# Expert weights in pieces for both experts of a pair, the overflow loop behind the second pair, and the transposed intermediate copied by ScalarE

## The chip, the core and the metric

One Trainium2 chip; the kernel runs on one of its cores. The metric is device time in microseconds (us) of one execution. Engines: PE is TensorE, PEld its weight loads, DVE is VectorE, ACT is ScalarE, POOL is GpSimd, SP is SyncE, which here issues nearly all DMAs.

## What is computed

One encoder layer on 512 tokens of width 2048: four mixers side by side (a differential attention, a bidirectional RWKV7, a dilated attention, an S5 scan), an output projection, cross attention, and a two-level mixture of experts; then a final RMS norm. The change touches only the mixture of experts. The reference of that part, cut to what matters:

```python
def hier_moe(h, wr_group, wr_expert, w1, w3, w2):
    gp = softmax(xt @ wr_group)            # 4 groups, the best one is taken
    ep = softmax(el)                       # 8 experts of that group, the best TOP_K = 2 are taken
    gate = (g_w * top_w).reshape(-1)
    ...
    def run(args):
        xb, e = args
        return (jax.nn.silu(xb @ w1[e]) * (xb @ w3[e])) @ w2[e]
    ...
    out = jnp.zeros((t, d), F32).at[slot_tok].add(ys.astype(F32) * slot_gate[:, None])
```

There are 32 experts; w1 and w3 are 2048x512 each, w2 is 512x2048, all in f32. So 12.6 MB of weights belong to an expert, and 402.7 MB to the stage.

## The kernel before, in words

The mixers and the cross attention come first and take the first 1736 us. The stage of the experts follows, in class `Moe`. `Moe.columns` runs beside the cross attention: it collects the router's logits `lg` while the last columns of the residual `H` are made. `Moe.run` then routes (`moe_route`), counts the tokens that go beyond 64 of an expert (`moe_overflow`), computes the gates (`gates`), and works through the experts in 16 pairs, `pair(mp, i, rest)` for i = 0 to 15. Each expert gets 64 slots, so a pair fills 128 partitions of PSUM with two matmuls of 64 columns of stationary weights that share the array.

A pair has these parts, in the order in which PE does them:

- 32 steps over w1 and w3 (into PSUM tiles `p1` and `p3`, both named `ph`), each of two matmuls (one per expert) of a channel tile `X[q, kt]` of 128 channels with a weight tile 128x512. An f32 matmul of this kind shows as two records in the trace.
- At step 10 `spread`: the one-hot of the slots is transposed and the gates are picked.
- `s` = silu(p1) * p3 (ACT at step 24, DVE after the last step), four transposes of `s` on PE into `ps`, and a copy of the transposed intermediate to SBUF, `hT` (named `mo_h`), on DVE (line 2067).
- w2 in four column blocks c of 512 (tile `py`), each followed by `split` (ACT writes `mo_yh`, DVE `mo_yl`) and, one block later, by `scatter`: eight matmuls that add the slots' results to token rows, and four DVE adds into the accumulator `mo_A` (line 2074). The scatter of the last block is handed to the next pair as `rest` and runs there after step 1.

The channel tiles X of a quad of experts (two pairs) come from `gather(q, u)`, u = 0 to 7: 16 matmuls of f32r halves of H (`mo_hi` from ACT, `mo_lo` from DVE, made by `halves`, two buffers each) with the one-hot of the quad's slots (`slots4`, DVE, line 1969), into one PSUM buffer (`pse`), which DVE then copies to `mo_xT` (line 1995). Four gathers for the next quad lie in each pair: three at the steps in `GQ`, one between the last step and the transposes.

Weights come through `Chunks`: pieces of 2 MB, one DMA each on SP's queue, into five buffers `wch` that are used in turn. `Chunks.order` is the order of the pieces; a piece holds eight channel tiles of one expert (w1, w3) or two column blocks of one expert (w2). SP waits, piece by piece, until PE is done with the buffer that it will overwrite:

```python
self.order += [(wn, 2 * i + j, h) for h in range(2) for wn in (1, 3) for j in range(2)]
self.order += [(2, 2 * i + j, h) for h in range(2) for j in range(2)]
```

As each step needs both experts, two pieces are in use at a time and are released together.

`moe_rest` is a loop for tokens beyond 64 slots (`tc.For_i(0, total, 1)`, line 1750), run by all engines: each loads `total`, compares and branches. For the inputs timed here the trace shows no instruction of its body. It stands between the routing and pair 0. The instructions' order on each engine is set by a scheduler from the code's order, its own time estimates and priorities (`tc.high_priority`), within the blocks that the loop separates.

Of the kernel before, what the change touches and what calls it, by code (L numbers as in the profile page):

```python
# [22 lines left out]
P = 128  # L23
# [60 lines left out]
def layouts(I):  # L84

    def tiles(w):
        n = w.shape[1] // P
        return np.ascontiguousarray(w.reshape(KT, P, n, P).transpose(2, 1, 0, 3).reshape(n, P, KT * P))  # L90
# [4 lines left out]
    def experts(w):  # L95
        return np.ascontiguousarray(w.reshape(32, KT, P, 512).transpose(0, 2, 1, 3)).reshape(32, P, KT * 512)

    def par(a):
# [6 lines left out]
        "moe_w2": np.ascontiguousarray(I["moe_w2"][0].reshape(32, 4, P, 2, 2, 512).transpose(0, 3, 2, 4, 1, 5)).reshape(32, 2, P, 4096),  # L105
# [1542 lines left out]
GQ = ((4, 12, 20), (18, 22, 28))  # L1648
# [94 lines left out]
def moe_rest(k, tc, pool, PS, H, A, G, rstd, VAL, blocks, gm, iota):  # L1743

    nc, I = k.nc, k.I
    ps, psh, psy = PS
    cum, cux, total = blocks
    total = nc.values_load(total[0:1, 0:1], min_val=0, max_val=NOV,
                           skip_runtime_bounds_check_because="1024 places make at most 15 blocks beyond the first 64 of an expert")
    with tc.For_i(0, total, 1) as i:  # L1750

        ib = pool.tile([P, 1], F32, name="ov_ib")
        nc.vector.tensor_copy(ib, iota[:, bass.ds(i, 1)])
        mk = pool.tile([P, NE + 1], F32, name="ov_mk")
        m2 = pool.tile([P, NE], F32, name="ov_m2")
# [7 lines left out]
        nc.vector.tensor_tensor(m2, mk[:, 0:NE], iota[:, 0:NE], op=OP.mult)  # L1763
        ef = pool.tile([P, 1], F32, name="ov_ef")
        nc.vector.tensor_reduce(ef, m2, axis=AX.X, op=OP.add)
        ei = pool.tile([P, 1], I32, name="ov_ei")
        nc.vector.tensor_copy(ei, ef)
        e = nc.values_load(ei[0:1, 0:1], engines=(mybir.EngineType.SP,), min_val=0, max_val=NE - 1,
                           skip_runtime_bounds_check_because="an index into 32 experts")
        pr = pool.tile([P, NT, NE], F32, name="ov_pr")  # L1770
        vs = pool.tile([P, NT], F32, name="ov_vs")
        gf = pool.tile([P, 2, NT], F32, name="ov_gf")
        for src, dst in ((VAL, vs), (G, gf[:, 0])):
            nc.vector.tensor_tensor(pr, src, bc(mk[:, None, 0:NE], [P, NT, NE]), op=OP.mult)
            nc.vector.tensor_reduce(dst, pr, axis=AX.X, op=OP.add)
        nc.vector.tensor_copy(gf[:, 1], rstd)
        nc.vector.tensor_scalar(vs, vs, mk[:, NE:NE + 1], None, op0=OP.subtract)
        OH = pool.tile([P, NT, SLOT], F32, name="ov_OH")
        nc.vector.tensor_tensor(OH, bc(iota[:, None, 1:], [P, NT, SLOT]), bc(vs[:, :, None], [P, NT, SLOT]), op=OP.is_equal)
        X = pool.tile([P, KT, SLOT], F32, name="ov_X")  # L1780
# [5 lines left out]
        OT = pool.tile([SLOT, NT, P], F32R, name="ov_OT")  # L1786
# [7 lines left out]
        g = pool.tile([SLOT, 2], F32, name="ov_g")  # L1794
        nc.vector.tensor_copy(g, pg[0:SLOT])
        hh = []
        for wn in (1, 3):
            p = psh.tile([P, DFF], F32, name="ph")
            for kt in range(KT):
                w = pool.tile([P, DFF], F32, name="ov_w", bufs=2)  # L1800
                nc.sync.dma_start(w, I[f"moe_w{wn}"][bass.ds(e, 1)].rearrange("e p c -> p (e c)")[:, kt * DFF:kt * DFF + DFF])
                mm(nc, p[0:SLOT], X[:, kt], w, start=(kt == 0), stop=(kt == KT - 1))
            hh.append(p)
        s = pool.tile([SLOT, DFF], F32, name="ov_s")
# [5 lines left out]
        hT = pool.tile([P, 4, SLOT], F32, name="ov_h")  # L1810
        nc.vector.tensor_copy(hT, pt)
        for c in range(4):
            py = psy.tile([P, 512], F32, name="py")
            for kt in range(4):
                w = pool.tile([P, DFF], F32, name="ov_w", bufs=2)
                a = ((c % 2) * 4 + kt) * DFF
                nc.sync.dma_start(w, I["moe_w2"][bass.ds(e, 1), c // 2].rearrange("e p c -> p (e c)")[:, a:a + DFF])
                mm(nc, py[0:SLOT], hT[:, kt], w, start=(kt == 0), stop=(kt == 3))
            yh = pool.tile([SLOT, 512], F32R, name="ov_yh")
            yl = pool.tile([SLOT, 512], F32R, name="ov_yl")  # L1820
# [9 lines left out]
class Moe:  # L1830
    def __init__(self, k, ctx, pool, H, tmp):
# [9 lines left out]
        nc.gpsimd.iota(self.iota, pattern=[[1, SLOT + 1]], base=0, channel_multiplier=0, allow_small_or_imprecise_dtypes=True)  # L1841
        self.lg = mp.tile([P, NT, 8 + NE], F32, name="mo_lg")
# [14 lines left out]
    def columns(self, c, tmp, ps, wr, t):  # L1857
# [4 lines left out]
        if c + t == 0:  # L1862
# [3 lines left out]
            nc.vector.tensor_tensor(wr, wr, bc(k.V[:, a:a + KT][:, :, None], [P, KT, NR]), op=OP.mult)  # L1866
        if (c, t) == (1, 0):
# [37 lines left out]
    def run(self, out, mx2):  # L1905
# [28 lines left out]
        for i in range(NE // 2 - 1):  # L1934
            rest = self.pair(mp, i, rest)

# [43 lines left out]
    def gather(self, q, u, ps=None, more=True):  # L1980
# [13 lines left out]
        k0 = 2 * u  # L1994
        nc.vector.tensor_tensor(self.piece[:, k0 % 4:k0 % 4 + 2], px, bc(self.gm[:, k0:k0 + 2][:, :, None], [P, 2, 4 * SLOT]), op=OP.mult)  # L1995
        if more:
            for j in range(2):
                self.halves((k0 + 2 + j) % KT)
# [27 lines left out]
    def pair(self, mp, i, rest=None, done=None):  # L2026
# [9 lines left out]
        todo = [] if q == NE // 4 - 1 else [lambda u=u: self.gather(q + 1, u, None, (q, u) != (NE // 4 - 2, 7))  # L2036
# [134 lines left out]
```

## Time and profile before

| | |
|---|---|
| median of 3 runs | 2807.52 us (2806.95 to 2813.43) |
| the profiled execution | 2806.31 us |
| its span, first to last instruction | 2804.6 us |
| PE busy over the span | 2647.6 us (94%) |
| mean granted TensorE clock | 0.983 of full speed |
| DMA, mean over the span | 227 GB/s; in the last thousand us near 400 GB/s |

The span is what the views of the trace count from; 1.7 us of the profiled execution's time lie outside it. A view is read as follows: "idle" is the time in which an engine did nothing before an instruction, with what ended it; a window's row gives each engine's busy time in it, then the clock, the share of time in which the 16 DMA engines were busy, and what they moved. Times in a timeline are us from the span's start.

### The profile page before, as it was taken

To read this page: it belongs to the slowest core of one execution; us is meant where nothing else is said; L and a number is where in the kernel's file an instruction comes from. 1 tells how busy PE (TensorE), PEld (TensorE's weight loads), DVE (VectorE), ACT (ScalarE), POOL (GpSimd) and SP (SyncE) were. 2 spreads that over 40 slices of the span, in tenths; PEclk is the share of its full clock that TensorE was granted. 3 is DMA by queue.
4 is the path that set the end of the run, shared out by engine and by line. 5 is a ranking of instruction groups with operands and counts; after the bars stand their busy time and mean duration, and the time that the engine had idled before them with its cause. 6 is when DMAs were issued, how large, how long until landed. Compare 5 with 4: busy or idle time off the path is not lost. (4 is left out here: it accounts for less than half of the span.)

```text
span 2804.6 us, 43696 instructions
## 1 busy us (share of the span) xinstructions
PE 2647.6 (94%) x17978; PEld 1803.4 (64%) x17978; DVE 1381.3 (49%) x2426; ACT 911.5 (32%) x1668; POOL 246.4 (9%) x370
## 2 busy tenths in 40 slices
PE   7999999999899799999999998999999999999996
PEld 4787777777678688788788777444444444444433
DVE  8747474655486564565434344333333333333323
ACT  4134333433266454656423343211111111111103
POOL 5300010000137800000000000000000000000000
PEclk9999999999999999999999999999999999999998
DMA  4521122221646577667534242689999999999997
GB/s 154 197 97 62 63 70 72 66 81 56 153 143 203 168 203 208 211 203 225 185 113 117 90 165 83 271 367 389 397 395 370 416 378 419 372 415 387 414 411 278
DMA packets 157420, 635.77 MB, mean 227 GB/s; under 512 B 25376, under 2 KB 58784, under 8 KB 132512
## 3 DMA queue, kind: packets, MB, share of 16 engines
q1 hardware_dynamic: 157216, 632.93, 61.1%
q8 instruction: 143, 2.34, 0.3%
q14 instruction: 61, 0.50, 0.1%
HBM read 593.55 MB, written 39.32 MB: 226 GB/s over the span
## 5 line engine op out<-in xcount | busy, mean ns | idle before, releaser
L1034 DVE TENSOR_TENSOR wlo<-wraw,whi 128x512 fp32r<-128x512 f32 x556 | 399.4, 725 | 387.0 <-ACT whi L1033 380.6
L1033 ACT CAST whi<-wraw 128x512 fp32r<-128x512 f32 x556 | 339.2, 620 | 579.3 <-PE pj L158 472.6
L158 PE MATMUL ph<-wch,mo_xT 128*64 128x512 f32 x2048 | 471.6, 599 | 11.2 <-DMA wch<-in_moe_w_dram 11.2
L158 PEld LDWEIGHTS ph<-wch,mo_xT 128*64 128x64 f32 x2048 | 149.0, 137 | 270.3 <-issue 237.1
L158 PE MATMUL pj<-xh,whi 128*128 128x512 f32 x688 | 294.0, 427 | 7.3 <-ACT xh L1036 6.7
L158 PE MATMUL pj<-xl,whi 128*128 128x512 f32 x688 | 273.6, 398 | 12.5 <-DVE xl L1037 12.5
L158 PE MATMUL pj<-xh,wlo 128*128 128x512 f32 x688 | 273.0, 397 | 6.5 <-DVE wlo L1034 6.5
L158 PE MATMUL py<-wch,mo_h 128*64 128x512 f32 (+1 forms) x1040 | 239.6, 605 | 23.9 <-DVE mo_h L2067 23.9
L2074 DVE TENSOR_TENSOR mo_A<-ps,mo_A 128x512 f32<-128x512 f32 (+1 forms) x260 | 163.4, 675 | 130.7 <-PE ps L2073 130.6
L1034 DVE TENSOR_TENSOR mo_lo<-H,mo_hi 128x512 fp32r<-128x512 f32 x128 | 87.8, 687 | 238.9 <-ACT mo_hi L1033 238.8
L1033 ACT CAST mo_hi<-H 128x512 fp32r<-128x512 f32 x128 | 79.3, 620 | 358.3 <-PE ps L158 358.3
L158 PEld LDWEIGHTS py<-wch,mo_h 128*64 128x64 f32 x1040 | 76.0, 139 | 160.3 <-issue 128.8
L158 PE MATMUL pj<-mh,wlo 128*128 128x256 f32 x512 | 148.6, 290 | 19.4 <-DVE wlo L1034 19.0
L158 PEld LDWEIGHTS pj<-xh,whi 128*128 128x128 f32 x688 | 130.9, 190 | 47.0 <-issue 11.7
L158 PEld LDWEIGHTS pj<-xl,whi 128*128 128x128 f32 x688 | 131.2, 191 | 42.6 <-DVE xl L1037 18.1
L158 PE MATMUL pj<-mh,whi 128*128 128x256 f32 x512 | 156.0, 305 | 2.5 <-ACT whi L1033 2.5
L158 PEld LDWEIGHTS pj<-xh,wlo 128*128 128x128 f32 x688 | 131.2, 191 | 38.3 <-DVE wlo L1034 10.2
L1036 ACT ACTIVATE mo_yh<-py,mo_g 128x512 fp32r<-128x512 f32 (+1 forms) x65 | 44.3, 682 | 318.1 <-PE py L158 318.1
L158 PE MATMUL pj<-ml,whi 128*128 128x256 f32 x512 | 147.0, 287 | 0.0
L158 PE MATMUL ps<-mo_OH,mo_hi 128*128 128x256 f32 x512 | 134.4, 299 | 10.6 <-DVE mo_gt L1044 8.9
L158 PEld LDWEIGHTS ps<-mo_OH,mo_hi 128*128 128x128 f32 x512 | 99.4, 194 | 61.2 <-issue 61.2
L158 PE MATMUL ps<-mo_OH,mo_lo 128*128 128x256 f32 x512 | 127.4, 286 | 0.0
(502 smaller groups left out, 4719.4 us busy)
## 6 DMA issues: line engine op xcount, KB each, us to landing
wch<-in_moe_w_dram SPq DMA_DIRECT2D x190, 2048.0 KB, 12.5
wraw<-in_w_in_dram SPq DMA_DIRECT2D x85, 512.0 KB, 3.8
wraw<-in_xa_wkv_dram SPq DMA_DIRECT2D x64, 512.0 KB, 4.7
wraw<-in_xa_wq_dram SPq DMA_DIRECT2D x32, 512.0 KB, 4.0
wraw<-in_xa_wo_dram SPq DMA_DIRECT2D x32, 512.0 KB, 5.0
wraw<-in_w_out_dram SPq DMA_DIRECT2D x32, 512.0 KB, 4.1
Ad<-kvo SPq DMA_DIRECT2D x32, 256.0 KB, 2.9
VWd<-kvo SPq DMA_DIRECT2D x32, 256.0 KB, 4.4
```

The lines of the kernel that those rows point to most:

```text
L158: nc.tensor.matmul(out, lhsT, rhs, start=start, stop=stop)
L1033: nc.scalar.copy(hi, x)
L1034: nc.vector.tensor_tensor(lo, x, hi.bitcast(F32), op=OP.subtract)
L1036: nc.scalar.activation(hi, x, AF.Copy, scale=scale)
L2074: nc.vector.tensor_tensor(A[:, t, c:c + n], pc, A[:, t, c:c + n], op=OP.add)
```

## The change

Three things, and what follows from them in the order of the work.

1. Pieces. The weights are laid out anew, and a piece of 2 MB now holds four channel tiles of both experts of a pair (w1, w3) or one column block of both experts (w2). Pieces of w1 and w3 alternate, and the 32 steps go over four channel tiles of w1, the same four of w3, the next four of w1 and so on.
2. The overflow loop stands behind pair 1, not before pair 0. `rest` of pair 1 is done before the loop, and five pieces are issued ahead of it. Its tiles share buffers with those of the pairs. `halves` of the first three channel tiles move into `columns` (three buffers instead of two), and the copy of the first gather (`keep`) is called after `gates`.
3. `hT` is copied by ACT at high priority. Of the four gathers of a pair two are at the steps in `GQ`, one before the transposes and one between the transposes and the first w2 block.

```diff
-        "moe_w2": np.ascontiguousarray(I["moe_w2"][0].reshape(32, 4, P, 2, 2, 512).transpose(0, 3, 2, 4, 1, 5)).reshape(32, 2, P, 4096),
+        "moe_w2": np.ascontiguousarray(I["moe_w2"][0].reshape(16, 2, 4, P, 4, 512).transpose(0, 4, 3, 1, 2, 5)).reshape(16, 4, P, 2, 2048),
...
-GQ = ((4, 12, 20), (18, 22, 28))
+GQ = ((8, 20), (14, 24))
...
+        if c == 2 and t < 3:
+            self.halves(t)
...
-        self.parts, self.X, self.gf = [], {}, []
         with pool("mr", 1, "right") as tmp:
-            for kt in range(2):
-                self.halves(kt)
             gates, self.VAL, pc = moe_route(k, self.mp, tmp, PS[0], self.lg, self)
             self.slots4(0)
-            self.gather(0, 0, PS[0])
-            blocks = moe_overflow(k, self.mp, tmp, pc, self.lim)
+            keep = self.gather(0, 0, PS[0])
+            self.blocks = moe_overflow(k, self.mp, tmp, pc, self.lim)
             gates()
+            keep()
         mx2.close()
-        with pool("ov", 1, "right") as ov:
-            moe_rest(k, tc, ov, PS, self.H, A, self.G, self.rstd, self.VAL, blocks, self.gm, self.iota)
...
             rest = self.pair(mp, i, rest)
+            if i == 1:
+                rest = rest()
+                self.load.ahead(self.load.n + sum(NCHUNK))
+                moe_rest(self, mp)
...
-        hi = self.hp.tile([P, NT, P], F32R, name="mo_hi", bufs=2)
-        lo = self.hp.tile([P, NT, P], F32R, name="mo_lo", bufs=2)
+        hi = self.mp.tile([P, NT, P], F32R, name="mo_hi", bufs=3)
+        lo = self.mp.tile([P, NT, P], F32R, name="mo_lo", bufs=3)
...
-        steps = [(h, pp, wn, kt) for h in range(2) for pp, wn in ((p1, 1), (p3, 3)) for kt in range(8 * h, 8 * h + 8)]
+        steps = [(pp, wn, kt) for g in range(0, KT, 4) for pp, wn in ((p1, 1), (p3, 3)) for kt in range(g, g + 4)]
...
-            if n == 24:
+            if n == 28:
                 nc.scalar.activation(s, p1, AF.Silu, scale=gr[:, 1:2])
-        nc.vector.scalar_tensor_tensor(s, p3, gr[:, 1:2], s, op0=OP.mult, op1=OP.mult)
+        with k.tc.high_priority(HP):
+            nc.vector.scalar_tensor_tensor(s, p3, gr[:, 1:2], s, op0=OP.mult, op1=OP.mult)
         hT = mp.tile([P, 4, P], F32, name="mo_h")
         if todo:
             todo.pop(0)()
         pt = ps.tile([P, 4, P], F32, name="ps")
         for kt in range(4):
             tr(nc, pt[:, kt], s[:, kt * P:kt * P + P], k.ident)
-        nc.vector.tensor_copy(hT, pt)
+        with k.tc.high_priority(HP):
+            nc.scalar.copy(hT, pt)
+        if todo:
+            todo.pop(0)()
...
-            self.order += [(wn, 2 * i + j, h) for h in range(2) for wn in (1, 3) for j in range(2)]
-            self.order += [(2, 2 * i + j, h) for h in range(2) for j in range(2)]
-        self.order[-2:] = [(0, i, c) for c in ((D - 1024, 512), (D - 512, 256), (D - 256, 256))]
+            self.order += [(wn, i, g, 512) for g in range(4) for wn in (1, 3)] + [(2, i, c, 512) for c in range(4)]
+        self.order[-1:] = [(2, i, 3, 256), (2, i, 3.5, 256)]
```

How the order moves, at the three places of which the prediction speaks. First PE behind the routing, where `mo_OH_18627` is the one-hot of the first quad and each gather ends in a matmul with `mo_lo`. Before, from the end of the first gather:

```order
L158 MATMUL ps<-mo_OH_18627,mo_hi 128x256
L158 MATMUL ps<-mo_OH_18627,mo_lo 128x256
L1748 TENSOR_LOAD mo_total
L1750 COMPARE_AND_BRANCH
L1750 UNCONDITIONAL_BRANCH x2
```

PE of the change, from the end of the second gather:

```order
L159 MATMUL ps<-mo_OH_18634,mo_hi 128x256
L159 MATMUL ps<-mo_OH_18634,mo_lo 128x256
L159 MATMUL ph<-wch,mo_xT 64x512 x4
L159 MATMUL ps<-mo_OH_18634,mo_hi 128x256
L159 MATMUL ps<-mo_OH_18634,mo_lo 128x256
```

The loop's load and branches are gone from this place; gathers and the first steps follow each other. Second DVE at the end of an odd pair (pair 3), where `mo_s` is the intermediate, `mo_xT` the copy of a gather and `mo_OH` (128x1024) the one-hot of the next quad. Before:

```order
L2060 SCALAR_TENSOR_TENSOR mo_s<-ph,mo_g,mo_s 128x512
L1034 TENSOR_TENSOR mo_lo<-H,mo_hi 128x512
L1995 TENSOR_TENSOR mo_xT<-ps,V 128x512
L1969 TENSOR_TENSOR mo_OH_20625<-mo_iota,mo_VAL 128x1024
L2067 COPY mo_h<-ps 128x512
```

The same place of the change, on DVE:

```order
L2074 SCALAR_TENSOR_TENSOR mo_s<-ph,mo_g,mo_s 128x512
L1035 TENSOR_TENSOR mo_lo<-H,mo_hi 128x512
L2011 TENSOR_TENSOR mo_xT<-ps,V 128x512
L1035 TENSOR_TENSOR mo_lo<-H,mo_hi 128x512 x2
L2011 TENSOR_TENSOR mo_xT<-ps,V 128x512
L1983 TENSOR_TENSOR mo_OH_20610<-mo_iota,mo_VAL 128x1024
```

The copy `mo_h` has left DVE, and a second gather's copy `mo_xT` stands there. ACT of the change, same pair (`mo_hi` are the halves for later gathers):

```order
L2072 ACTIVATE mo_s<-ph,mo_g 128x512
L1034 CAST mo_hi<-H 128x512 x2
L2082 COPY mo_h<-ps 128x512
L1034 CAST mo_hi<-H 128x512 x2
L1037 ACTIVATE mo_yh<-py,mo_g 128x512 x4
```

The copy stands on ACT behind two casts of halves. Third SP around the loop, where `mo_total` is the loop's bound and `wch` a piece. Before:

```order
L2132 DMA wch<-in_moe_w_dram 128x4096 x3
L1097 DMA wraw<-VWd 128x2x512 x13
L2132 DMA wch<-in_moe_w_dram 128x4096 x2
L1748 TENSOR_LOAD mo_total
L1750 COMPARE_AND_BRANCH
```

SP of the change there:

```order
L2141 DMA wch<-in_moe_w_dram 128x4096 x3
L1098 DMA wraw<-VWd 128x2x512 x13
L2141 DMA wch<-in_moe_w_dram 128x4096 x26
L1751 TENSOR_LOAD mo_total
L1753 COMPARE_AND_BRANCH
```

29 pieces stand before the loop instead of 5: the 24 of pairs 0 and 1 and five more.

## Rows read from the trace of the kernel before

**Rows 1.** PE's waits, 1750 us to the end: total us, times, longest us

```profile
PE py L158 <- DVE mo_h L2067: 23.9, 16, 2.3
PE ph L158 <- DMA wch<-in_moe_w_dram: 11.2, 9, 2.7
```

**Rows 2.** PE's waits, 1850 to 2670 us: the pairs 1 to 13

```profile
PE py L158 <- DVE mo_h L2067: 21.2, 13, 2.3
```

**Rows 3.** Windows: length, busy PE, PEld, DVE, ACT, POOL, then clock, DMA share, GB/s

```profile
1975.00:2600.00 625.00, 603.54 (x2938) 275.98 (x2936) 227.50 (x366) 89.34 (x139) 0.00 (x0) 0.99 0.96 395
2650.00:2700.00 50.00, 45.28 (x196) 16.46 (x195) 12.18 (x21) 2.66 (x5) 0.00 (x0) 0.97 1.01 424
```

**Rows 4.** Timeline, end of pair 3: start us, us, engine, line, operation [idle before]

```profile
2003.18 0.60 PE L163 MATMUL ps<-ident,mo_s 128*128 128x128 f32 x4
2003.57 0.68 DVE L1995 TENSOR_TENSOR mo_xT<-ps,V 128x512 f32<-128x512 f32 x1
2004.17 1.22 DVE L1969 TENSOR_TENSOR mo_OH<-mo_iota,mo_VAL 128x1024 fp32r<-128x1024 f32 x1
2005.31 0.68 DVE L2067 COPY mo_h<-ps 128x512 f32<-128x512 f32 x1
...
2006.05 7.09 PE L158 MATMUL py<-wch,mo_h 128*64 128x512 f32 x32 [2.26 <-DVE mo_h L2067]
```

**Rows 5.** Timeline, end of pair 4, and ACT's copy of the same form (groups by line)

```profile
2067.27 0.68 DVE L2067 COPY mo_h<-ps 128x512 f32<-128x512 f32 x1
...
2068.00 7.09 PE L158 MATMUL py<-wch,mo_h 128*64 128x512 f32 x32 [1.12 <-DVE mo_h L2067]
...
L1882 ACT COPY mo_hT<-ps 128x512 f32<-128x512 f32 x8 | 4.7, 587 | 16.7 <-PE ps L163 16.7
```

**Rows 6.** Timeline: w2 blocks after a wait, pair 5; steps and w2 blocks of pair 14

```profile
2133.25 8.78 PE L158 MATMUL py<-wch,mo_h 128*64 128x512 f32 x32 [2.25 <-DVE mo_h L2067]
...
2692.55 8.78 PE L158 MATMUL ph<-wch,mo_xT 128*64 128x512 f32 x30 [2.73 <-DMA wch<-in_moe_w_dram]
2703.68 8.78 PE L158 MATMUL py<-wch,mo_h 128*64 128x512 f32 x32 [0.78 <-DVE mo_h L2067]
```

**Rows 7.** The tile wch, 1757 to 1800 us: its DMAs, first issue, and landing

```profile
L2132 SPq DMA_DIRECT2D wch<-in_moe_w_dram x6: 328/354/435, 1775.4 to 1796.9; - x6
...
DMA to landing us min/median/max: 7.3/11.7/15.5
```

**Rows 8.** Timeline around the routing and the loop

```profile
1737.16 1.29 DVE L1034 TENSOR_TENSOR mo_lo<-H,mo_hi 128x512 fp32r<-128x512 f32 x2 [0.47 <-ACT mo_hi L1033]
...
1753.26 0.29 DVE L1721 TENSOR_TENSOR mo_G<-mo_a,mo_a 128x128 f32<-128x128 f32 x1
1754.46 1.28 ACT L1043 ACT_TABLE_LOAD   x1 [5.26 <-DVEq L1750]
...
1757.53 0.58 PE L158 MATMUL ps<-mo_OH,mo_hi 128*128 128x256 f32 x1 [8.92 <-DVE mo_gt L1044]
```

**Rows 9.** Timeline, end of pair 3: the last w2 block and the adds into mo_A

```profile
2021.01 3.65 PE L158 MATMUL py<-wch,mo_h 128*64 128x512 f32 x16
...
2025.98 0.74 DVE L1037 SCALAR_TENSOR_TENSOR mo_yl<-py,mo_g,mo_yh 128x512 fp32r<-128x512 f32 x1
...
2026.63 1.88 DVE L2074 TENSOR_TENSOR mo_A<-ps,mo_A 128x512 f32<-128x512 f32 x3
...
2029.43 2.48 DVE L2074 TENSOR_TENSOR mo_A<-ps,mo_A 128x512 f32<-128x512 f32 x4 [0.92 <-PE ps L2073]
```

**Rows 10.** The chain that ended last, in order of time: gathers (ps), first steps (ph)

```profile
1757.53 3.78 PE ps L158 x16
...
1763.47 2.11 PE ps L158 x16
...
1961.40 1.87 PE ph L158 x8
...
2473.85 1.87 PE ph L158 x8
```

More of the change, by code (lines that the diff above doesn't have):

```diff
@@ L1740, in moe_overflow, with moe_rest @@
     return cum, cux, total
[L1743 to L1747, printed above, removed]
+def moe_rest(mo, mp):
+    k, H, A = mo.k, mo.H, mo.A
+    nc, tc, I = k.nc, k.tc, k.I
+    ps, psh, psy = mo.PS
+    iota, gm = mo.iota, mo.gm
+    cum, cux, total = mo.blocks
     total = nc.values_load(total[0:1, 0:1], min_val=0, max_val=NOV,
@@ L1762, in moe_rest @@
         nc.vector.tensor_scalar(mk[:, NE:], mk[:, NE:], 1.0, float(SLOT), op0=OP.add, op1=OP.mult)
[L1763 to L1766, printed above, removed]
-        nc.vector.tensor_copy(ei, ef)
[L1768 to L1773, printed above, removed]
+        ef = mp.tile([P, 2], F32, name="ov_ef")
+        for j in range(2):
+            nc.vector.tensor_tensor(m2, mk[:, 0:NE], mo.which[:, j], op=OP.mult)
+            nc.vector.tensor_reduce(ef[:, j:j + 1], m2, axis=AX.X, op=OP.add)
+        ei = mp.tile([P, 2], I32, name="ov_ei")
+        nc.vector.tensor_copy(ei, ef)
+        e, o = [nc.values_load(ei[0:1, j:j + 1], engines=(mybir.EngineType.SP,), min_val=0, max_val=n - 1,
+                               skip_runtime_bounds_check_because="an index into 16 pairs of experts") for j, n in ((0, NE // 2), (1, 2))]
+        pr = mp.tile([P, NT, NE], F32, name="ov_pr")
+        vs = mp.tile([P, NT], F32, name="ov_vs")
+        gf = mp.tile([P, 2, NT], F32, name="ov_gf")
+        for src, dst in ((mo.VAL, vs), (mo.G, gf[:, 0])):
             nc.vector.tensor_tensor(pr, src, bc(mk[:, None, 0:NE], [P, NT, NE]), op=OP.mult)
             nc.vector.tensor_reduce(dst, pr, axis=AX.X, op=OP.add)
-        nc.vector.tensor_copy(gf[:, 1], rstd)
+        nc.vector.tensor_copy(gf[:, 1], mo.rstd)
         nc.vector.tensor_scalar(vs, vs, mk[:, NE:NE + 1], None, op0=OP.subtract)
-        OH = pool.tile([P, NT, SLOT], F32, name="ov_OH")
+        OH = mo.hp.tile([P, NT, SLOT], F32, name="ov_OH", tag="mo_OH", bufs=2)
         nc.vector.tensor_tensor(OH, bc(iota[:, None, 1:], [P, NT, SLOT]), bc(vs[:, :, None], [P, NT, SLOT]), op=OP.is_equal)
-        X = pool.tile([P, KT, SLOT], F32, name="ov_X")
+        X = mo.hp.tile([P, KT, SLOT], F32, name="ov_X", tag="mo_xT", bufs=6)
         for kt in range(KT):
@@ L1993, in gather @@
             self.piece = X
[L1994 to L1998, printed above, removed]
+        k0, X = 2 * u, self.piece
+        for n in range(KT * q + k0 + 3, min(KT * q + k0 + 5, KT * NE // 4)):
+            self.halves(n % KT)
+        return lambda: nc.vector.tensor_tensor(X[:, k0 % 4:k0 % 4 + 2], px, bc(self.gm[:, k0:k0 + 2][:, :, None], [P, 2, 4 * SLOT]), op=OP.mult)
     def factors(self, mp):
@@ L2035, in pair @@
         p3 = psh.tile([P, DFF], F32, name="ph")
-        todo = [] if q == NE // 4 - 1 else [lambda u=u: self.gather(q + 1, u, None, (q, u) != (NE // 4 - 2, 7))
-                                            for u in range(4 * b, 4 * b + 4)]
-        steps = [(h, pp, wn, kt) for h in range(2) for pp, wn in ((p1, 1), (p3, 3)) for kt in range(8 * h, 8 * h + 8)]
+        todo = [] if q == NE // 4 - 1 else [lambda u=u: self.gather(q + 1, u)() for u in range(4 * b, 4 * b + 4)]
+        steps = [(pp, wn, kt) for g in range(0, KT, 4) for pp, wn in ((p1, 1), (p3, 3)) for kt in range(g, g + 4)]
         first = [(0, u) for u in range(1, 8)] if i == 0 else []
-        oh = self.slots(i)
         s = mp.tile([P, DFF], F32, name="mo_s")
-        for n, (h, pp, wn, kt) in enumerate(steps):
+        for n, (pp, wn, kt) in enumerate(steps):
             if first and wn == 1 and kt % 2 == 0:
-                self.gather(*first.pop(0), ps)
+                self.gather(*first.pop(0), ps)()
             for j in range(2):
@@ L2051, in pair @@
                 self.factors(mp)
-            if n == 10:
+            if n == 4:
+                oh = self.slots(i)
+            if n == 11:
                 OT, gr = self.spread(mp, i, oh)
-            if n == (0 if i else 30) and todo and b == 0:
+            if n == (4 if i else 30) and todo and b == 0:
                 self.slots4(q + 1)
```

67 lines of the change are left out of this document (35 added, 32 removed).

## The prediction

> **What bounds the kernel now.** I read four views of the last 1050 us, the stage of the experts, since the change leaves the rest as it is. The windows come first: over 625 us of the steady pairs PE is busy 603.5 us, so 97%, and the DMA engines are busy 96% of the time [rows 3]. Two resources are nearly full, so the next question is which one waits for the other. The view of PE's waits answers it: from 1750 us on, PE waits 23.9 us in 16 waits for `mo_h`, the copied intermediate, and only 11.2 us in 9 waits for a weight piece [rows 1]. PE sets the pace, and its own chain (transposes, copy, w2) is the largest hole. The chain in order of time gives the pace: from the start of pair 3 to that of pair 11 are 2473.85 - 1961.40 = 512.5 us, 64.1 us for each of 8 pairs [rows 10]. The timeline of the end of a pair shows why the hole has two sizes: in odd pairs DVE does a gather's copy and a one-hot of 1.22 us before `mo_h`, and PE idles 2.26 us [rows 4]; in even pairs there is no one-hot and it is 1.12 us [rows 5].
>
> How much room the DMA has is to be seen where it was full without a break: 424 GB/s between 2650 and 2700 us [rows 3]. A piece of 2.097 MB then takes 4.95 us, the 12 pieces of a pair 59.4 us. PE without its holes needs about 603.5 / 625 x 64.1 = 61.9 us, a little less at full clock. So PE stays the bound, with some 2 us a pair to spare: that is the key number of this prediction.
>
> **The change, part by part.**
>
> *The copy on ACT and the gather behind the transposes.* What PE waits for after the transposes is now covered by a gather, 2.11 us of PE work [rows 10]. ACT's copy of that form takes 0.59 us against DVE's 0.68 [rows 5, 4]; behind two casts of halves, which need PE's gather before the transposes, it ends some 1.4 us after it begins to be possible, inside the gather. But the gather needs `pse`, which DVE must first have emptied from the gather before: in rows 4 this copy ends at 2004.25, 0.47 us after the transposes (2003.78). The order on DVE in front of it is the same in the change, so I put 0.45 us where 2.26 or 1.12 us were. The waits of pairs 0 to 13 are 21.2 us for pairs 1 to 13 [rows 2] and 1.1 for pair 0; 14 x 0.45 = 6.3 us remain: a gain of **16.0 us** (from 7, if 1.1 us stays in each pair, to 22). Pairs 14 and 15 have no gather and keep their 0.8 us.
>
> *Pieces for both experts.* Before, a pair of pieces is held for 16 matmuls, which leaves three buffers for loading; now one piece is held for 8 matmuls and four buffers are ahead. The 8 pieces of w1 and w3 are eaten in 8 x 3.58 (half of a 7.09 us block of 32 records [rows 4]) + 2 gathers + a scatter + the spread, about 36 us, and loaded in 39.6; the four of w2 are eaten in about 26 us and loaded in 19.8. A lead of four pieces swings by one. I take all **11.2 us** of the waits for pieces [rows 1] as gone (from 0 to 11.2). In pairs 14 and 15, without gathers, PE needs 53 to 55 us against 59.4: a full lead of 20 us covers the 10 us that they lack together. On the rate, "DMA: Bandwidth & Descriptors" of the Trainium skill, section "Where 436 GB/s comes from", says that a core's HBM traffic binds at about 358 GB/s. By that a piece would take 5.86 us and a pair 70 us, longer than pairs take now, and nothing could be gained; the trace's 395 GB/s over 625 us speaks against it, so it gets no chance.
>
> *The clock.* After some of these holes PE runs a block at half speed: 32 records take 8.78 us in place of 7.09 [rows 6, 4]. I count five such blocks (at 1877, 2133 and 2389 us, and two in pair 14 behind a wait of 2.73 us for a piece [rows 6]), 1.7 us each. Without the holes I take them as gone: **8.5 us** (from 0 to 8.5).
>
> *The start.* Two halves (1.29 us of DVE and 0.47 of waiting before the routing's first operation [rows 8]) move into the cross attention, where DVE has time: **1.7 us**. Without the loop PE need not idle 8.92 us [rows 8] nor do the second gather at half clock, 3.78 us for 2.11 [rows 10]. What limits it now is DVE: halves, the first gather's copy, then overflow and gates. With DVE's present durations I get the first four steps at 1752.2 and the third gather at 1754.2 us, against 1763.47 [rows 10]: **9.2 us** (from 4, if the factors' wait for POOL and ACT holds DVE up, to 11).
>
> *The loop behind pair 1.* This is the added wait. All engines meet at it. From the end of the last w2 block (2024.66 in pair 3), DVE still has `mo_yl` and adds, with 3 + 4 adds left after `mo_yl` (to 2026.72 + 1.88 + 2.48 = 2031.1 [rows 9]), so 6.4 us. From DVE's last operation before the loop to PE's next instruction after it took 1757.53 - 1753.55 = 4.0 us [rows 8]. PE's own work in these 10.4 us is two scatters, 4.2 us; 6.2 idle and about 2 us of half clock make a cost of **8 us** (from 4 to 14). Behind the waiting SP the pieces stand still; five were issued, so PE starts with full buffers, and the DMA's pause of some 7 us comes out of its spare time.
>
> The rest costs nothing: POOL's two small index rows lie in its idle time, and the moved silu and one-hots lie beside the steps.
>
> **The sum.** 16.0 + 11.2 + 8.5 + 1.7 + 9.2 - 8.0 = 38.6 us from the profiled execution's 2806.3: 2767.7. The median of the runs is 1.2 us above that execution, so **2769 us**, 1.4% less.
>
> **The rivals.**
>
> *The DMA becomes the bound* (0.20). Over the steady pairs 395 GB/s at a busy share of 0.96 is 411 GB/s when busy [rows 3], not 424. Then a pair's pieces take 61.2 us, as long as PE, and the waits for pieces and the slow blocks in pair 14 come back: 11.2 + 3.4 us, so 2784 us. For it: the share never was 1.00 for 600 us. Against: at full queues it reads 424.
>
> *The seams cost more* (0.12). `pse` is empty 0.65 us later in each of 14 pairs (9 us), and the loop costs 14 us in place of 8: 2784 us. For it: DVE does everything in order, and the loop's drain is only modelled.
>
> *Pieces one behind the other* (0.06), the slower side. Before, two pieces are issued together, so one is always queued behind the other. Now one piece is issued at each release, and a piece alone takes 7.3 us from issue to landing [rows 7]. If SP's issue falls behind so that often only one is on its way, a piece costs between 4.95 and 7.3 us. The 187 pieces after the first five now have from 1775 [rows 7] to about 2762 us, 5.3 us each; from there on the change is slower, and at 5.5 us per piece it ends at 2807 + 187 x 0.2 = 2844 us. Against it: once PE waits, four buffers are free and four pieces are queued, which restores the rate.
>
> *The change does not do what it says* (0.04). The copy on ACT comes late behind casts that wait for the second gather, and the pieces were late for another reason: then only the start and the loop count, 2807.5 - 1.7 - 9.2 + 8 = 2805 us, no change.
>
> **How the numbers follow.** My forecast has 0.58. Its own bounds give 2755 to 2782; the DMA and the seams reach to 2784, both together to 2798. With 2752 to 2798 about 0.85 is in. About 0.3% (8 us) is what a measurement of this kernel can tell from no change. Faster by more than that: 0.58 + 0.20 + 0.12 = 0.90; within it 0.04; slower 0.06.
>
> **What would show it.** PE's waits for `mo_h` from 23.9 to about 2 us, with a new wait of some 0.45 us a pair before the gather behind the transposes, on DVE's `mo_xT`; pairs of 61.5 to 62 us; no wait for pieces in pairs 14 and 15; one hole of 6 us behind pair 1, with half clock behind it; the third gather about 9 us earlier. I am wrong if PE waits for pieces by more than 15 us in all, or if pairs still take over 63 us.

## The result, and the profile after

The change makes the kernel **1.7% faster**: a median of 2760.53 us (2759.32 to 2764.0, 4 runs) against 2807.23 us of the kernel before, measured beside it; the ratio is 0.9832, with a 95% interval of 0.9814 to 0.9851. That is 46.7 us. The forecast was 2769 us, with a sum of 38.6 us gained; direction and range hold. But two terms of the sum came out far from their size, one came near by luck, and one was missing; that is what the experiments show.

PE's waits in the profiled execution of the changed kernel (2760.12 us, span 2758.4), from 1740 us to the end: what waited, for whom, total us, times, longest us.

```profile
PE ph L159 <- SPq L1753: 6.2, 1, 6.2
PE ps L159 <- ACT mo_h L2082: 4.6, 7, 0.7
PE ph L159 <- DVE mo_xT L2011: 4.3, 1, 4.3
PE ps L159 <- DVE mo_xT L2011: 4.3, 7, 0.6
PE ph L159 <- DMA wch<-in_moe_w_dram: 2.7, 3, 1.2
...
PE py L159 <- ACT mo_h L2082: 1.3, 2, 0.7
...
PE py L159 <- DMA wch<-in_moe_w_dram: 0.3, 1, 0.3
```

Beside [rows 1]: the 23.9 us for `mo_h` are 1.3 us in pairs 14 and 15, plus 4.6 + 4.3 = 8.9 us in front of the gather behind the transposes (14 waits of 0.64 us; 0.45 was forecast). The waits for pieces went from 11.2 to 3.0 us (2.7 and 0.3), all in pair 15. The first line is the loop behind pair 1, the third the start.

The windows that answer to [rows 3]: length, busy PE, PEld, DVE, ACT, POOL, granted clock, DMA share, GB/s.

```profile
1975.00:2600.00 625.00, 618.64 (x3074) 277.27 (x3072) 228.36 (x368) 97.01 (x153) 0.00 (x0) 1.00 0.98 413
2650.00:2700.00 50.00, 48.40 (x222) 18.27 (x220) 13.73 (x23) 7.38 (x10) 0.00 (x0) 1.00 1.01 428
```

PE does 5% more matmuls in the same 625 us, at full clock, and the transfers run at 413 GB/s in place of 395. The chain that ended last, beside [rows 10], gives the pace: (2443.70 - 1955.03) / 8 = 61.1 us per pair in place of 64.1.

```profile
1955.03 1.87 PE ph L159 x8
...
2443.70 1.87 PE ph L159 x8
```

The timeline of the end of a pair, beside [rows 4], shows what PE now waits for: start us, us, engine, line, operation, and in brackets the idle time before it.

```profile
1992.00 0.60 PE L164 MATMUL ps<-ident,mo_s 128*128 128x128 f32 x4
...
1992.38 0.68 DVE L2011 TENSOR_TENSOR mo_xT<-ps,V 128x512 f32<-128x512 f32 x1
1992.63 0.59 ACT L2082 COPY mo_h<-ps 128x512 f32<-128x512 f32 x1
...
1993.21 0.36 PE L159 MATMUL ps<-mo_OH,mo_hi 128*128 128x256 f32 x1 [0.61 <-DVE mo_xT L2011]
```

Two things end at nearly one time, at 1993.06 DVE's emptying of `pse` and at 1993.22 ACT's copy. PE idles 0.61 us in front of the gather, and behind it the w2 block starts without a wait. That it is the emptying for which the gather waits, E3 and E8 show below.

How the runs are compared below: up to the routing the program hardly changes, but that part alone differs by some us from one execution to the next (in runs of nearly the same code the routing's first matmul lies between 1733.4 and 1743.1 us). So beside the times I give the **stretch from the routing's first matmul to the last instruction**, in which every kernel here issues the same number of matmul records. The window of that stretch in the kernel before, with the columns as above:

```profile
1742.81:2804.60 1061.79, 995.41 (x4838) 454.13 (x4838) 386.54 (x646) 164.22 (x277) 1.27 (x3) 0.98 0.91 375
```

And in the changed kernel:

```profile
1738.03:2758.40 1020.37, 975.18 (x4838) 439.05 (x4838) 375.54 (x629) 172.12 (x292) 1.28 (x3) 0.99 0.94 390
```

So 41.4 us are won behind the routing, 4.8 us ahead of it. "Lost at half clock" below is half the time in which the granted clock was 0.50, summed from windows of 2.5 us over this stretch without its first 30 and last 40 us: 8.5 us before, 3.4 after. The sums also count half clock in which PE idles, behind the loop above all (1.7 of the 3.4 us after, 3.3 us in E1, 2.4 in E6), so differences between them are good to about 1.5 us. Stretches, waits and clock are those of one profiled execution of each kernel.

### The profile page after: what moved, and what is told of

Its sections match the earlier page's. It is cut to its first block, busy times and chain, and to the rows that moved or that the text cites. A ratio compares the mean times of both kernels' runs of the same rounds, so it can differ in the third digit from the quotient of the medians.

```text
span 2758.4 us, 43705 instructions
## 1 busy us (share of the span) xinstructions
PE 2626.8 (95%) x17978; PEld 1787.7 (65%) x17978; DVE 1369.7 (50%) x2410; ACT 919.3 (33%) x1683; POOL 250.1 (9%) x372
## 5 line engine op out<-in xcount | busy, mean ns | idle before, releaser
L159 PE MATMUL ph<-wch,mo_xT 128*64 128x512 f32 x2048 | 460.0, 599 | 13.2 <-SPq L1753 6.2
L159 PEld LDWEIGHTS ph<-wch,mo_xT 128*64 128x64 f32 x2048 | 140.3, 137 | 278.9 <-issue 264.5
L159 PE MATMUL py<-wch,mo_h 128*64 128x512 f32 (+1 forms) x1040 | 231.0, 590 | 1.7 <-ACT mo_h L2082 1.3
L159 PEld LDWEIGHTS py<-wch,mo_h 128*64 128x64 f32 x1040 | 70.3, 136 | 133.8 <-issue 127.8
```

What stands on the lines that cost most here:

```text
L159: nc.tensor.matmul(out, lhsT, rhs, start=start, stop=stop)
```

## The experiments

Eleven kernels ran. E1 to E4 shared one set of runs of the kernel before, E5 to E8 another, E9 to E11 a third, so ratios are compared, not times.

| | what differs | median us | ratio to before, 95% | stretch us |
|---|---|---|---|---|
| changed kernel | | 2760.53 | 0.9832 (0.9814 to 0.9851) | 1020.4 |
| E1 | old pieces | 2801.99 | 0.9977 (0.9957 to 0.9996) | 1062.0 |
| E2 | no gather behind the transposes | 2768.08 | 0.9850 (0.9824 to 0.9875) | 1028.0 |
| E3 | copy on DVE | 2765.97 | 0.9838 (0.9813 to 0.9862) | 1022.6 |
| E4 | loop before pair 0 | 2757.13 | 0.9808 (0.9783 to 0.9833) | 1016.1 |
| E5 | before, with the new pieces alone | 2791.47 | 0.9939 (0.9918 to 0.9960) | 1041.7 |
| E6 | both parts of the copy undone | 2791.47 | 0.9946 (0.9928 to 0.9964) | 1048.8 |
| E7 | no loop | 2750.35 | 0.9803 (0.9779 to 0.9827) | 1011.8 |
| E8 | E4, late gather in `ps` | 2745.17 | 0.9777 (0.9758 to 0.9795) | 1007.2 |
| E9 | halves late | 2764.45 | 0.9831 (0.9810 to 0.9853) | 1021.3 |
| E10 | E9, halves in the old pool | 2770.86 | 0.9852 (0.9828 to 0.9875) | 1022.9 |
| E11 | E8, second gather ahead of the loop | 2746.0 | 0.9770 (0.9752 to 0.9788) | 1005.4 |

**E1, the old pieces.**

```diff
-        steps = [(pp, wn, kt) for g in range(0, KT, 4) for pp, wn in ((p1, 1), (p3, 3)) for kt in range(g, g + 4)]
+        steps = [(pp, wn, kt) for h in range(2) for pp, wn in ((p1, 1), (p3, 3)) for kt in range(8 * h, 8 * h + 8)]
...
-            self.order += [(wn, i, g, 512) for g in range(4) for wn in (1, 3)] + [(2, i, c, 512) for c in range(4)]
+            self.order += [(wn, 2 * i + j, h) for h in range(2) for wn in (1, 3) for j in range(2)]
+            self.order += [(2, 2 * i + j, h) for h in range(2) for j in range(2)]
```

> The changed kernel with the weights in the pieces of before (eight channel tiles or two column blocks of one expert; 16 steps of w1 and w3 in blocks of eight); copy, gathers, start and loop stay as changed. Theory (the new pieces release one buffer at a time, which keeps four ahead): PE's waits for pieces come back, 11 us as in the kernel before or more, since PE now asks for a pair in 61 us, with 3 to 4 us of half clock behind them: 2772 to 2780 us, some 15 us slower than the changed kernel. Rival (the holes at the copy made the pieces late, and they are gone): within 3 us of the changed kernel's 2760.5, waits for pieces under 4 us.

Measured: 0.9977. Behind the routing nothing is left of the gain (1062.0 us, before 1061.8), although the waits for the copy stay as short as in the changed kernel. PE's waits in E1 from 1740 us:

```profile
PE ph L159 <- DMA wch<-in_moe_w_dram: 20.1, 10, 2.7
PE ph L159 <- SPq L1753: 9.8, 1, 9.8
PE ps L159 <- ACT mo_h L2080: 4.6, 7, 0.7
...
PE py L159 <- DMA wch<-in_moe_w_dram: 0.4, 1, 0.4
```

Its window of the steady pairs, where the transfers reach 400 GB/s at a share of 0.98:

```profile
1975.00:2600.00 625.00, 607.60 (x2966) 279.98 (x2966) 225.44 (x362) 94.28 (x149) 0.00 (x0) 0.99 0.98 400
```

Waits for pieces are 20.5 us, 17.5 more than with the new ones; the loop's hole is 3.6 us longer; 13.5 us are lost at half clock, 10.1 more. That makes 31.2 of 41.6 us. The other 10 to 12 lie in PE's *busy* time (995.85 us, after 975.18, less the clock), which neither theory had. Where they come from is to be seen in the kernel before, in the timeline of PE around one wait for a piece (the bracket is PE's idle time and what ended it):

```profile
2230.29 5.36 PE L158 MATMUL ph<-wch,mo_xT 128*64 128x512 f32 x22
2236.47 2.79 PE L158 MATMUL ph<-wch,mo_xT 128*64 128x512 f32 x10 [0.82 <-DMA wch<-in_moe_w_dram]
```

These 32 records take 5.36 + 2.79 = 8.15 us beside the wait; 32 records in one piece take 7.09 [rows 4]. The cut lies behind 22 records, five steps and a half: step 16 has done its matmul for the first expert, and the piece of the second is late. Two matmuls that share the array run side by side (in the trace their records start 0.01 us apart); cut apart, each runs alone. So a late piece of one expert costs 1.06 us more than its wait. All nine waits for pieces before and all eleven in E1 cut a step in this way. With the new pieces a wait falls between steps, never inside one. What such a wait costs is to be seen in pair 15 of the changed kernel, in the timeline of PE:

```profile
2716.60 3.65 PE L159 MATMUL py<-wch,mo_h 128*64 128x512 f32 x16 [0.68 <-ACT mo_h L2082]
2720.60 3.65 PE L159 MATMUL py<-wch,mo_h 128*64 128x512 f32 x16 [0.35 <-DMA wch<-in_moe_w_dram]
```

Cut between steps, the 32 records take 3.65 + 3.65 = 7.30 us beside the wait, only 0.21 more than in one piece. So 0.85 of the 1.06 us come from the place of the cut and not from the wait as such. ("TensorE: Matmul & The Clock Gate" of the Trainium skill, section "Part 3: Packing small matmuls — row/col tiling", says that small matmuls in different parts of the array run concurrently; the rows show what is lost when they can't.) No run changed the place of this cut alone.

**E2 and E3, one part of the copy undone at a time.** E2 has three gathers at steps and none behind the transposes, with the copy on ACT; E3 has the copy on DVE, with the gather behind it.

```diff
-GQ = ((8, 20), (14, 24))
+GQ = ((8, 14, 20), (14, 20, 26))
...
             nc.scalar.copy(hT, pt)
-        if todo:
-            todo.pop(0)()
```

> The changed kernel with three gathers at steps of each pair and one before the transposes, none behind them; the copy stays on ScalarE at high priority. Theory (what fills the hole is the gather behind the transposes): PE waits for the copy in each of 14 pairs, 1.1 to 1.7 us, in place of 0.64 before the gather; with 0 to 5 us of half clock behind these holes 2767 to 2780 us. Rival (the engine and the priority of the copy bring the gain): waits of 0.7 us as in pairs 14 and 15, so within 2 us of 2760.5.

```diff
         with k.tc.high_priority(HP):
-            nc.scalar.copy(hT, pt)
+            nc.vector.tensor_copy(hT, pt)
```

> The changed kernel with the copy of the transposed intermediate on VectorE, still at high priority and with the gather behind the transposes. Theory (the gather covers the copy, whoever makes it): 0.68 us on VectorE behind the gather's copy ends inside the gather's 2.1 us; PE's waits stay at 0.6 us a pair, only pairs 14 and 15 wait 0.1 us longer: 2760 to 2763 us. Rival (the copy on ScalarE is what matters): waits for mo_h of 1 us and more in each pair, 2772 us and more.

Measured: E2 0.9850, E3 0.9838, both intervals overlapping the changed kernel's. In E2 the wait for the copy is 10.8 us in 16 waits, 0.68 us each, so my theory falls there, and the rival holds for the waits but not for the time; the stretch is 7.6 us longer, of which I can name 1.7 us of half clock, 2.0 of waits for pieces and 0.8 of waits for the copy and the loop; the rest, 3 us, lies in PE's busy time. It is there in all three kernels with the new pieces and no gather behind the transposes: PE's busy time, less what half clock took of it, is 971.4 to 972.1 us in E2, E5 and E6, and 966.1 to 969.5 in those with that gather. Why stays open. In E3 the theory holds: 8.9 us in 14 waits, the same as in the changed kernel. PE's waits of E2:

```profile
PE py L159 <- ACT mo_h L2082: 10.8, 16, 0.7
```

PE's waits of E3:

```profile
PE ps L159 <- DVE mo_xT L2011: 8.9, 14, 0.7
```

The timeline of E3 at the end of pair 3:

```profile
1998.45 0.68 DVE L2011 TENSOR_TENSOR mo_xT<-ps,V 128x512 f32<-128x512 f32 x1
1999.05 0.68 DVE L2082 COPY mo_h<-ps 128x512 f32<-128x512 f32 x1
1999.28 0.36 PE L159 MATMUL ps<-mo_OH,mo_hi 128*128 128x256 f32 x1 [0.61 <-DVE mo_xT L2011]
```

The gather starts at 1999.28, while the copy still runs (to 1999.73): it waits for the emptying of `pse`, which ends at 1999.13, and not for the copy. So each part alone is nearly enough. In E2 ACT's copy ends 0.6 us behind the transposes; in the changed kernel the gather, held by `pse`, starts no sooner.

**E6, both parts undone** (copy on DVE in its turn, three gathers at steps; the product before the transposes also loses its priority).

> The changed kernel with both parts of the copy undone: VectorE makes it, in its turn without priority, three gathers of a pair at steps and one before the transposes. Theory after the two single undoings (either part alone leaves some 0.65 us a pair, so each is enough): with neither, VectorE's gather copy stands in front and PE waits 1.1 us in each of 16 pairs, 17 to 20 us in all against 10.2: 2767 to 2772 us. Rival (the prediction's term in full, with holes of 2.3 us in odd pairs and half clock behind some): waits of 24 us, 2776 us and more.

Measured: 0.9946, the rival. PE's waits in E6:

```profile
PE py L159 <- DVE mo_h L2081: 23.9, 16, 2.3
```

DVE's timeline in E6 at the end of an odd pair, and PE's next row:

```profile
2123.57 0.69 DVE L2011 TENSOR_TENSOR mo_xT<-ps,V 128x512 f32<-128x512 f32 x1
2124.17 1.22 DVE L1983 TENSOR_TENSOR mo_OH<-mo_iota,mo_VAL 128x1024 fp32r<-128x1024 f32 x1
2125.30 0.69 DVE L2081 COPY mo_h<-ps 128x512 f32<-128x512 f32 x1
...
2126.04 1.86 PE L159 MATMUL py<-wch,mo_h 128*64 128x512 f32 x4 [2.25 <-DVE mo_h L2081]
```

All 23.9 us are back, to the tenth [rows 1], since the one-hot stands in front of the copy again. Behind the holes of 2.25 us PE falls to half clock: 15.3 us are lost, 11.9 more than in the changed kernel. 13.7 us of waits and 11.9 of clock are 25.6 of the 28.4 us. This profiled execution is the fastest of E6's four, 7.5 us under their median; by the ratios of all runs the two parts are worth 32 us.

**E5, the new pieces alone**, in the kernel before.

> The kernel before with the new pieces and the order of steps that goes with them, and nothing else of the change. Theory A (pieces and copy need each other: without the old pieces the waits for pieces go, the holes at the copy stay): PE's waits for pieces under 4 us, for the copied intermediate still 20 us or more, half-clock blocks behind those holes; 15 to 22 us faster than the kernel before, a ratio of 0.992 to 0.995. Theory B (since the old pieces alone took back everything, the new ones alone bring nearly everything): 32 us or more faster, a ratio of 0.9885 or less. Rival (pieces bring nothing while the holes are there): within 5 us of the kernel before.

Measured: 0.9939, theory A. PE's waits in E5:

```profile
PE py L158 <- DVE mo_h L2072: 23.9, 16, 2.3
...
PE ph L158 <- DMA wch<-in_moe_w_dram: 3.2, 3, 1.3
```

The window of its stretch:

```profile
1749.23:2790.90 1041.67, 984.24 (x4838) 440.05 (x4838) 386.48 (x646) 164.12 (x277) 1.27 (x3) 0.98 0.93 382
```

20.1 us of stretch: 7.8 of waits for pieces (11.2 to 3.4, with 0.2 us in front of w2) and 11.2 of PE's busy time (995.4 to 984.2), with as much lost at half clock as before, 8.5 us. With nine waits for pieces in [rows 1] the cut steps, at 1.06 us each, account for 9.5 of these 11.2. E1 and E5 together say how the parts combine: behind the routing the rest of the change alone is worth 0, the pieces alone 20, both 41 us. The ratios of all runs, which take in the part ahead of the routing, give 6, 17 and 47 us. Shorter holes alone only make PE ask sooner for pieces that are late.

**E4 and E7, the loop.** E4 calls `moe_rest` before pair 0; E7 leaves it out, and with it the work for tokens beyond 64 of an expert.

```diff
             rest = self.pair(mp, i, rest)
-            if i == 1:
-                rest = rest()
-                self.load.ahead(self.load.n + sum(NCHUNK))
-                moe_rest(self, mp)
```

> The changed kernel with the overflow loop back before pair 0; all else as changed. Theory by the sum of the prediction (9.2 us gained at the start, 8 paid behind pair 1): 2760.5 + 1.2 = 2762 us (2757 to 2767); PE idles some 6 us less behind pair 1 and 5 to 9 us more at the start. Rival A (behind pair 1 the loop costs nothing net): 2769 us and more. Rival B (it is dearer behind pair 1, because PE has work to lose there and none at the start): 2755 us or less.

> The changed kernel without the overflow loop (the work for tokens beyond 64 of an expert is left out; with these inputs there is none). Theory (behind pair 1 the loop costs PE's idle time of 6.2 us and some 2 us of half clock, and the pause of the transfers comes out of their spare time): 8 us less, 2752 us. Rival (the pause is paid once more by later pieces): 2748 us or less. With the loop before pair 0 at 2757, this also tells what it costs there: 5 us by the theory.

Measured: the stretch is 1020.4 with the loop behind pair 1, 1016.1 before pair 0, 1011.8 without. So it costs **8.6 us behind pair 1 and 4.3 us at the start**: rival B in direction, and the move loses 4.3 us. Against E7, PE idles 4.6 us more over the stretch in E4, and 6.9 us more in the changed kernel, with 1.7 us of its busy time lost at half clock. The ratios of all runs give 8 us behind pair 1 and 1.4 at the start, with intervals that overlap; the price at the start rests on one execution of each kernel. The changed kernel's timeline at the loop:

```profile
1885.05 4.27 DVE L2091 TENSOR_TENSOR mo_A<-ps,mo_A 128x512 f32<-128x512 f32 x7
...
1887.92 0.39 PE L2090 MATMUL ps<-mo_yl,mo_OT 128*128 128x512 f32 x1
1894.32 1.29 DVE L1975 TENSOR_TENSOR mo_OH<-mo_iota,mo_VAL 128x512 bf16<-128x512 f32 x2 [5.00 <-SPq L1753]
```

DVE's last add ends at 1889.32, and then no engine shows an instruction for 5.00 us. What the engines wait for is to be seen on SP's queue, which stands at the loop's line; its wait in the changed kernel:

```profile
SPq L1753 <- SPq L1753: 9.0, 1, 9.0
```

The timeline of SP's queue there, with the last of the pieces issued ahead:

```profile
1883.13 0.33 SPq L2141 DMA_DIRECT2D wch<-in_moe_w_dram  x1
```

The tile wch from 1883 to 1884 us, its DMA's time to landing:

```profile
DMA to landing us min/median/max: 10.1/10.1/10.1
```

This piece lands at 1893.2; there SP's wait ends, and DVE goes on 1.1 us later. The DMA view of these 10 us (1885 to 1895), the busy share in tenths, 0.25 us a digit, shows the queues running empty before (a packet counts where it starts):

```profile
DMA  9999969979797997997996150030100000000210
```

The same view of E1 (1885 to 1895), where DVE idles 8.69 us and goes on at 1896.63:

```profile
DMA  4939969397796959979397893947969141431100
```

There the last piece goes out at 1882.16 as the second of two, needs 13.3 us and lands at 1895.5, again 1.1 us ahead of DVE. In all seven kernels profiled with the loop behind pair 1 (the changed one, E1 to E3, E6, E9, E10) the distance is 1.1 us, and DVE's idle time 4.2 to 8.7 us. With the loop before pair 0 the queues are empty, and ScalarE goes on 0.4 us after DVE's last operation. So the loop is left only when the last piece in flight has landed. That the engines' code comes late does not fit: the last packets that bring it end 0.8 to 2.7 us ahead of DVE, at no fixed distance. Whether fewer pieces ahead of the loop would shorten the hole, no run tested.

At the start there is also less to lose: the first steps wait for DVE's `mo_xT` without any loop, because DVE's chain of routing, overflow, gates and copy ends last. PE's wait there in E7, without the loop:

```profile
PE ph L159 <- DVE mo_xT L2007: 4.1, 1, 4.1
```

And in E4, with the loop before pair 0, where the whole hole comes in front of the second gather:

```profile
PE ps L159 <- DVE mo_gt L1045: 8.5, 1, 8.5
```

**E9 and E10, the halves, and where they lie.** In the profile ahead of the routing something stood out that the prediction had not looked at: the kernel before waits in its cross attention, the changed one doesn't. PE's wait in the kernel before:

```profile
PE pj L158 <- ACT whi L1033: 3.9, 1, 3.9
```

The wait of SP's queue that leads to it:

```profile
SPq L2132 <- PE pj L158: 8.7, 1, 8.7
```

Before, the first three weight pieces wait 8.7 us until PE has read the scores' operands, are issued at 1617.26 us, and stand just ahead of a raw weight that the cross attention needs (issued at 1618.76). After, they wait for nothing there and go out at 1611.53, early enough. No line of the diff speaks of this; but the tiles of the halves moved from one pool to another, and with them the places of what is allocated after. E9 computes the halves at the start of the routing again, in the new place; E10 also puts the tiles back in the pool `mo1`. The order of instructions is the same in both.

```diff
-        if c == 2 and t < 3:
-            self.halves(t)
...
         with pool("mr", 1, "right") as tmp:
+            for kt in range(3):
+                self.halves(kt)
```

```diff
-        hi = self.mp.tile([P, NT, P], F32R, name="mo_hi", bufs=3)
-        lo = self.mp.tile([P, NT, P], F32R, name="mo_lo", bufs=3)
+        hi = self.hp.tile([P, NT, P], F32R, name="mo_hi", bufs=3)
+        lo = self.hp.tile([P, NT, P], F32R, name="mo_lo", bufs=3)
```

> The changed kernel with the halves of the first three channel tiles computed at the start of the routing again, in tiles that stay where the change puts them (pool mo, three buffers). Theory of the prediction (two halves cost 1.7 us there; three about 2.4): the routing's first operation 1.8 to 2.5 us later, no other difference: 2762 to 2763 us. In the cross attention PE does not wait for whi, as in the changed kernel. Rival (the wait of 3.9 us for whi in the kernel before came from the halves' place in time): that wait is back.

> The same with the tiles of the halves in the pool mo1, where the kernel before has them; the order of instructions on every engine is that of the run above, only addresses differ. Theory (where the first three weight pieces come to lie decides when they may be loaded: over the operands of the scores they wait for PE and are issued just ahead of a raw weight of the cross attention): the three pieces are issued some 6 us later, PE waits 3.9 us for whi with some 1.8 us of half clock behind it: 5 to 6 us slower than the run above. Rival (that wait is chance from run to run): no wait for whi, the same time as the run above within 2 us.

Measured in E10, PE's wait:

```profile
PE pj L159 <- ACT whi L1034: 4.2, 1, 4.2
```

The wait of SP's queue in E10:

```profile
SPq L2141 <- PE pj L159: 8.7, 1, 8.7
```

Both waits are back by the place of these tiles alone, with the same order of instructions on PE, DVE, ACT and POOL in the two traces; E9 has neither. Of the thirteen kernels the three with the halves in the old pool (before, E5, E10) wait for `whi` here, 3.9 to 4.2 us, and the other ten do not. That the pieces then come to lie over the scores' operands is read from what SP waits for; the traces show no addresses. From the first matmul of the cross attention's value product (with `xa_ph`) to the routing E10 takes 127.2 us (1622.1 to 1749.32), E9 119.7 (1625.5 to 1745.18), the changed kernel 117.3 (1620.7 to 1738.03), the kernel before 125.0 (1617.8 to 1742.81). So the address is worth 7.5 us between E9 and E10 in this stretch (6.4 in the medians, whose intervals overlap); three halves cost 2.4 us, as expected; and of the 7.7 us between before and after, two halves take 1.8 (PE's wait in front of the routing's first matmul is 6.4 us before, 4.6 after) and the address the other 5.9.

**E8 and E11, a faster version.** E8 is E4 with the gather behind the transposes in a buffer of `ps`.

```diff
-        todo = [] if q == NE // 4 - 1 else [lambda u=u: self.gather(q + 1, u)() for u in range(4 * b, 4 * b + 4)]
+        todo = [] if q == NE // 4 - 1 else [lambda u=u: self.gather(q + 1, u, ps if u % 4 == 3 else None)() for u in range(4 * b, 4 * b + 4)]
```

> The changed kernel with the loop back before pair 0 and with the gather behind the transposes written to one of the three buffers of ps in place of the single pse. Theory (the 0.64 us in front of that gather is the wait for pse to be emptied): these waits, 8.9 us in 14 pairs, go; against 2757 with the loop there: 2748 to 2751 us. Rival (the transfers are the bound at 61 us a pair): the same time comes back as waits for pieces, 2755 us or more.

Measured: 2745.17 us, ratio 0.9777, faster than both kernels; its stretch is 8.9 us shorter than E4's, which is what PE waited in front of the gathers. So those waits were for `pse`. Its window of 625 us:

```profile
1975.00:2600.00 625.00, 625.00 (x3125) 282.95 (x3125) 234.87 (x378) 99.53 (x157) 0.00 (x0) 1.00 0.99 418
```

PE has no idle time left there, and the DMA share is 0.99: both are full, and a pair takes 60.2 us. E11 adds the second gather ahead of the loop:

```diff
             self.blocks = moe_overflow(k, self.mp, tmp, pc, self.lim)
+            keep1 = self.gather(0, 1, PS[0])
             gates()
             keep()
```

> The kernel with the loop before pair 0 and the gather behind the transposes in ps, and in addition the second gather ahead of the loop, where PE waits anyway (8.2 us). Theory (PE's time in front of the loop is free; VectorE's extra casts and copy hold the loop up by 1 to 2 us): the gather's 2.1 to 3.8 us come off, 1 to 2 are given back: 2743 us (2741 to 2746). Rival (VectorE's chain to the loop sets the start): 2745 to 2748 us.

Measured: 2746.0 us, ratio 0.9770, not to be told from E8. The stretch of the one profiled execution is 1.8 us shorter; that is inconclusive.

## Why the prediction was right, and where it was not

The sum was 38.6 us; the profiled executions differ by 46.2. Term by term:

- **The copy and the clock** (16.0 + 8.5 = 24.5): right in mechanism and nearly in size. E6 gives 28.4 us (32 by the ratios), and the 23.9 us of waits with the half-clock blocks behind them return as read. The remaining wait is 0.64 us a pair, not 0.45. It is for `pse`, as forecast (E3, E8), and `pse` is empty 0.46 us after the transposes, as forecast; but the gather starts 0.15 us after that, for which the term had nothing. That the gather covers the copy was not needed: on ACT the copy ends 0.6 us after the transposes with or without it (E2).
- **The pieces** (11.2): mis-sized. Alone they are worth 20.1 us (E5; 17 by the ratios), and without them nothing else counts behind the routing (E1). Two steps failed. Late pieces cost PE busy time too, 11.2 us here, which a list of waits can't show; and "PE without its holes needs 61.9 us" a pair was taken from a stretch that contained these cut steps and slow blocks. It needs 483.6 / 8 = 60.4 us (PE busy in the eight pairs of the chain). I also added the terms as if they were independent; with the old pieces the shorter holes turn into waits for the transfers, 20.5 us in all, and a pair takes 63.2 us (E1).
- **The start** (1.7 + 9.2): too large. The halves are right, at 1.8 us. But I get 1752.2 us from [rows 8] only with the halves already taken off, so the 1.7 us were counted twice. From the routing to the third gather it is 15.2 us (1738.03 to 1753.19) in place of 20.7, so 5.5 gained; and E7 and E4 put the price of the loop at the start at 4.3, not 9.2.
- **The loop behind pair 1** (-8): right in size, 8.6 us, with the forecast 6.2 us of idle time, but by luck. The order in which I had it (DVE's drain, then 4.0 us) left out the pieces in flight: SP's queue stands at the loop until the last one has landed, 3.9 us after DVE's last add. And the 4.0 us were read where PE waited for `mo_gt`, not for the loop; ScalarE went on 0.9 us after DVE's last operation there [rows 8]. Moving the loop was a loss of 4.3 us, where the sum had a gain of 1.2.
- **Not in the sum**: the address of the first three pieces, 5.9 us. The sentence that the change leaves the rest as it is was wrong: the pieces' place changed when they could start (E10). Against it, the changed kernel's profiled execution reached the cross attention's value product 2.9 us later than that of before.

So the nearness of the total is partly luck: 19 us too little for pieces (8.9), copy (3.9) and address (5.9) stand against 5 too much at the start and the 2.9 us of a later beginning. The other 3 us I cannot place: the terms were measured one at a time, and they overlap.

The rivals: the **DMA as the bound** did not come with the new pieces (share 0.98, waits 3.0 us); with the old ones PE waits 20.5 us for it in E1, and in E8 it is as full as PE. Against the 358 GB/s of "DMA: Bandwidth & Descriptors" of the Trainium skill (section "Where 436 GB/s comes from") the measurement decides again, with 413 GB/s over 625 us on this one core. Of the **seams**, the wait for `pse` is 0.19 us longer than forecast, not the 0.65 that the rival named, and the loop cost 8.6, not 14. **Pieces one behind the other** and **no effect** are ruled out.

## What to carry to other kernels

Before adding up terms, ask what each resource would be waiting for if the other terms came true: here shorter holes were worth 0 without a loading order that releases one buffer at a time, and 21 us with it. Cut transfers along the unit that the work consumes together; where two matmuls share the array, a piece that is late for one of them costs the other's company as well. And when tiles change pools, look at who else's buffers move: a tile's place decided when three loads could start, and that was worth more than the code that was moved (5.9 us against 1.8).

## What the runs showed of the hardware that was not expected

- A wait that cuts apart two matmuls that share the array lengthens PE's busy time: 32 records took 8.15 us beside the wait, where 7.09 is usual, and 7.30 with a wait between two steps.
- A loop of zero trips kept all engines idle until 1.1 us after the last piece in flight had landed, in each of seven kernels: 4.2 to 8.7 us of DVE's time, against 0.4 us until the first engine went on where no transfer was on its way. The price in time was 8.6 us in the middle of the work and 4.3 us at the start.
- At 418 GB/s over 625 us the transfers kept a DMA share of 0.99 while PE was busy for all 625.00 us at full clock (E8), without one wait for a piece.
